# Who issues the last store of a chunked WKV kernel, and how its last logarithm is cut

## The chip, the core and the metric

The kernel runs on one core of one Trainium2 chip. The core has a matmul engine (TensorE, PE in the profile), a vector engine (VectorE, DVE), an activation engine (ScalarE, ACT), a general engine (GpSimd, POOL) and SyncE (SP), which here issues transfers and waits for them. Transfers between the on-chip memory and DRAM run on the core's 16 DMA engines; in this kernel SP, ACT and POOL all issue some. The metric is the device time of one execution in microseconds (us), lower is better.

## The reference

For each of 16 sequences and each of 256 channels a recurrence runs over 2048 steps. It keeps a weighted sum `aa` of values, a weighted sum `bb` of weights, and their common exponent `pp`:

```python
for t in range(seq_len):
    kk, vv = k[b, t, :], v[b, t, :]
    ww = u + kk
    qq = np.maximum(pp, ww)
    e1, e2 = np.exp(pp - qq), np.exp(ww - qq)
    output[b, t, :] = (e1 * aa + e2 * vv) / (e1 * bb + e2 + 1e-08)
    ww = pp - w + kk
    qq = np.maximum(ww, kk)
    e1, e2 = np.exp(ww - qq), np.exp(kk - qq)
    aa, bb, pp = e1 * aa + e2 * vv, e1 * bb + e2, qq
```

The output is a quotient, numerator over denominator, for every sequence, step and channel: 33.55 MB of float32, and as much again is read for each of `k` and `v`.

## The kernel before

**Tiling.** Time is cut into 16 chunks of 128 steps, and in each chunk the 16 sequences are taken four at a time. Such a piece of work, four sequences by 128 steps by 256 channels, is called a pair, since it is held as two halves `i` of two sequences each. There are `NP = 64` pairs, numbered in the order in which they run; the last one is 63. A tile of a pair has 128 partitions (steps) and 2 halves of 512 columns (two sequences by 256 channels).

**Stages of a pair.** `k` and `v` are loaded; matmuls form exponents in a PSUM tile `X` (lines 200 and 206), ScalarE takes exponentials (line 209), VectorE multiplies by `v` (line 218). Column sums go through a small state computation once per chunk, which carries the recurrence from chunk to chunk. Then the output side starts, and it is this side that the change touches:

- `DEN`: 12 matmuls (`apply`, line 321) form the denominator in a tile `X`, four for each of three terms, half 0 ahead of half 1 within each term.
- `LN`: `log_den` takes the logarithm of the whole tile on ScalarE (line 329) into a tile `rd`.
- `INV`: `inverse` takes exp(-x) of `rd` on ScalarE (line 337), which gives one over the denominator. `parts(n)` gives one slice with both halves for all pairs but the last, and two slices, one for each half, for pair 63.
- `NUM`: 12 more matmuls form the numerator, in a tile `num` or `X`.
- `MUL`: `mult` multiplies numerator and inverse on VectorE (line 349) into the output tile `ot`, again by `parts(n)`.
- `ST`: `store` issues, from SP, a transfer of half 0 (256 KB, line 362) and then a first piece of half 1 (128 KB, `piece`, line 355). Half 1 is stored in two pieces, since its two groups of 64 steps lie in swapped partitions.
- `SQ`: `store_rest` issues the second piece of half 1 (128 KB, also line 355). This step exists for pairs for which `shared(n)` is true, among them all from pair 52 on; for those the piece is issued by POOL.

**Order of the work.** The order of instructions on each engine is not left to a scheduler. Every step has a place on a common axis (the table `P`, with own entries under `TAIL` for the last ten pairs), steps are emitted by place as soon as those they name are done, and `K` keeps each engine's instructions in that order. In the last pairs ScalarE's order is strictly LN, INV of one pair, then LN, INV of the next.

**The end.** The program closes (line 478, where the tile context ends) with a drain instruction on each engine and a barrier: SP waits for the landing of all transfers, reports to a semaphore, and POOL, which has drained as the others have, waits for all reports, clears the semaphores and releases the engines.

Of the kernel before, what the change touches and what calls it, by code (L numbers as in the profile page):

```python
# [7 lines left out]
F32 = mybir.dt.float32  # L8
# [3 lines left out]
ACT = mybir.ActivationFunctionType  # L12
# [3 lines left out]
def kernel(  # L16
# [9 lines left out]
    K = tc.keep_in_program_order  # L26
    PE, DVE, SC, POOL, SP = nc.tensor, nc.vector, nc.scalar, nc.gpsimd, nc.sync
# [5 lines left out]
    D = 2 * Dm  # L33
    NP = 4 * NST
# [9 lines left out]
    RS = 2.0 ** -20  # L44
# [26 lines left out]
    rpool = ctx.enter_context(tc.tile_pool(name="rpool", bufs=NRD))  # L71
# [117 lines left out]
    X = [psx.tile([128, 2, D], F32, tag=f"X{a}", name=f"X{a}") for a in range(2)]  # L189
# [119 lines left out]
    RD, NUM, OT = {}, {}, {}  # L309
# [14 lines left out]
    def den(n, a):  # L324
        apply(X[a], n, ("S", "Id"), 1)

    def log_den(n, a):
        rd = rpool.tile([128, 2, D], F32, tag="rd", name="rd")
        K(SC.activation(rd, X[a], ACT.Ln, scale=RS))  # L329
        RD[n] = rd  # L330

    def parts(n):
        return (slice(0, 1), slice(1, 2)) if n == NP - 1 else (slice(0, 2),)

    def inverse(n):
        for i in parts(n):
            K(SC.activation(RD[n][:, i], RD[n][:, i], ACT.Exp, scale=-1.0))  # L337

    def by_x(n):
        return n >= NP - XT and n % 2 == 1  # L340
# [11 lines left out]
    def piece(n, h, queue):  # L352
        c, p = divmod(n, 4)
        t0 = c * TC + HS * (1 - h)
        K(queue.dma_start(out=out[4 * p + 2:4 * p + 4, t0:t0 + HS, :].rearrange("n t d -> t n d"), in_=OT[n][HS * h:HS * h + HS, 2:4, :]))
# [8 lines left out]
            piece(n, h, SP)  # L364

    def store_rest(n):
        piece(n, 1, POOL)


    ops, free = {}, {"K": NK, "KP": NKP, "V": NV, "N": 1, "RD": NRD, "OT": NOT, "VB": NVB}  # L370
# [5 lines left out]
    for n in range(NP):  # L376
# [24 lines left out]
        if j == 3:  # L401
            s = P["STATE"][0 if c == 0 else 2 if c == NST - 1 else 1]
            for i, (name, fn, *after) in enumerate((
# [5 lines left out]
                if not (name in ("SN", "KP") and c + 1 == NST):  # L409
                    step((name, c), n + s[i] - lead * SHARE, fn, (c,), after, mode=1)  # L410
        step(("DEN", n), place("DEN"), den, (n,), [("BK", c), ("DEN", n - 1), "mats"], "X", mode=3)
        step(("LN", n), place("LN"), log_den, (n,), [("DEN", n), ("INV", n - 1)], "RD", ["X"])
        step(("INV", n), place("INV"), inverse, (n,), [("LN", n)])
        step(("NUM", n), place("NUM"), num, (n,), [("BK", c), ("TV", n), ("NUM", n - 1), "mats"], "X" if by_x(n) else "N", mode=3)
        step(("MUL", n), place("MUL"), mult, (n,), [("NUM", n), ("INV", n), ("MUL", n - 1)], "OT", ["X" if by_x(n) else "N", "RD"])
        step(("ST", n), place("ST"), store, (n,), [("MUL", n), ("ST", n - 1)], None, [] if shared(n) else ["OT"])
        if shared(n):
            step(("SQ", n), place("SQ"), store_rest, (n,), [("ST", n)], None, ["OT"])
# [64 lines left out]
```

## Time and profile before

| what | us |
|---|---|
| median of 3 runs (lowest to highest) | 292.77 (292.13 to 294.27) |
| the profiled execution, its own time | 293.15 |
| its span, first to last instruction | 291.4 |
| time of the profiled execution outside the span | 1.75 |

The mean granted TensorE clock of the profiled execution is 0.992. All times inside the trace count from the start of the span. In the rows, a name like SPq or POOLq is an engine's sequencer, which issues transfers, waits and drains; L355 is line 355 of the kernel before. A row of a timeline or of the chain of waits begins with its start and its length in us. A row of a line's instructions has its shortest, median and longest duration in ns and then the starts of the first and last of them in us.

### The profile page before, as it was taken

The page shows a single profiled execution, that of the slowest core. Times are in us where ns is not written, and L with a number is a line of the kernel's source. Part 1 is how long each engine was busy: PE and PEld are TensorE (multiplying, and loading weights), DVE is VectorE, ACT ScalarE, POOL GpSimd, SP SyncE. Part 2 cuts the span into 40 slices and gives each one's busy share as a digit, 9 for nine tenths or more (in the row PEclk, how much of TensorE's full clock was granted, in tenths as well). Part 3 has the DMA queues.
Part 4 walks back from the last instruction along what each step waited for, and adds up shares of the span by engine and source line. Part 5 has one row for each costly group of instructions (what it writes and reads, how often), then busy time and mean ns, then how long its engine had stood idle before and what let it go on. Part 6 is the DMA issues. An engine that isn't in the chain of part 4 may idle for free.

```text
span 291.4 us, 8084 instructions
## 1 busy us (share of the span) xinstructions
PE 273.7 (94%) x3275; PEld 140.6 (48%) x3275; DVE 247.1 (85%) x423; ACT 258.4 (89%) x290; POOL 175.7 (60%) x218
## 2 busy tenths in 40 slices
PE   7999999999999999999999999999999999997750
PEld 7545744454545545444545455444545444544330
DVE  6575769989897989989898989899898989797860
ACT  1486398999999999999999999999999999997890
POOL 6177349575767687575767686675757674422230
PEclk9999999999999999999999999999999999999996
DMA  7999999999999999999999999999999999965885
GB/s 220 348 279 351 346 350 291 377 377 390 378 400 381 389 392 373 392 368 398 382 390 389 394 390 379 394 374 391 367 394 373 390 387 393 315 189 165 243 248 143
DMA packets 58550, 101.21 MB, mean 347 GB/s; under 512 B 5128, under 2 KB 43536, under 8 KB 58512
## 3 DMA queue, kind: packets, MB, share of 16 engines
q0 software_dynamic: 21216, 65.54, 65.0%
q1 hardware_dynamic: 37280, 35.14, 35.9%
q8 instruction: 25, 0.41, 0.6%
q14 instruction: 13, 0.11, 0.1%
q10 hardware_dynamic: 16, 0.01, 0.0%
HBM read 67.12 MB, written 33.55 MB: 345 GB/s over the span
## 4 chain that ended last, share of the span: by engine, by line
PE 71%; DMA 7%; DVE 5%; issue 5%; POOL 5%; ACT 4%; POOLq 0%; SPq 0%; ACTq 0%; DVEq 0%
PE X L206 17%; PE X L321 15%; PE num L321 12%; PE X L200 10%; PE TURN L148 9%; PE TOT L244 6%; DMA kf<-in_k_dram 4%; POOL vr L114 2%; DMA WUf<-in_u_dram 2%; PE TOT L257 2%; DVE ot L349 2%; POOL kr L110 2%; ACT EZR L209 1%; ACT rd L329 1%; DVE EZR L218 1%
## 5 line engine op out<-in xcount | busy, mean ns | idle before, releaser
L209 ACT ACTIVATE EZR<-X 128x1024 bf16<-128x1024 f32 x128 | 126.8, 1014 | 14.7 <-PE X L206 14.6
L213 POOL CAST vb<-vr 128x1024 bf16<-128x1024 f32 x54 | 56.3, 1043 | 70.9 <-DVE EZR L218 68.1
L218 DVE TENSOR_TENSOR EZR<-EZR,vb 128x2048 bf16<-128x2048 bf16 x64 | 77.9, 1219 | 0.4 <-ACT EZR L209 0.2
L349 DVE TENSOR_TENSOR ot<-num,rd 128x1024 f32<-128x1024 f32 x60 | 73.2, 1221 | 4.5 <-ACT rd L337 3.2
L337 ACT ACTIVATE rd<-rd 128x1024 f32<-128x1024 f32 (+1 forms) x65 | 67.9, 1046 | 2.0
L329 ACT ACTIVATE rd<-X 128x1024 f32<-128x1024 f32 x64 | 65.6, 1025 | 3.2 <-PE X L321 1.6
L148 PE MATMUL TURN<-Z 128*128 128x192 bf16 x331 | 57.0, 262 | 1.6 <-DVE Z L132 1.6
L114 POOL DMA_DIRECT2D vr<-in_v_dram x61 | 46.2, 758 | 13.8 <-DVE kr L193 7.1
L148 PEld LDWEIGHTS <-Z 128*128 128x128 bf16 x331 | 30.1, 102 | 49.0 <-issue 47.1
L200 PE MATMUL X<-WU,CO 64*64 64x512 bf16 x512 | 51.9, 390 | 0.9 <-DVE WU L175 0.6
L206 PE MATMUL X<-kr,NLE 128*128 128x512 f32 x128 | 45.6, 438 | 0.0
L206 PE MATMUL X<-kr,NLZ 128*128 128x512 f32 x128 | 45.5, 437 | 0.0
L107 POOL DMA_DIRECT2D kf<-in_k_dram x53 | 40.2, 758 | 0.0
L193 DVE CAST kr<-kf 128x1024 fp32r<-128x1024 f32 x39 | 31.9, 845 | 5.5 <-DMA kf<-in_k_dram 5.3
L200 PEld LDWEIGHTS <-CO 64*64 64x64 bf16 x512 | 15.7, 105 | 31.1 <-issue 26.2
L321 PE MATMUL X<-EZR,S 64*64 64x512 bf16 x256 | 26.2, 394 | 1.7 <-ACT rd L329 1.0
L321 PE MATMUL X<-cb,Id 64*64 64x512 bf16 x256 | 25.8, 376 | 0.0
L321 PE MATMUL X<-EZR,Id 64*64 64x512 bf16 x256 | 25.8, 376 | 0.0
L321 PE MATMUL num<-EZR,SN 64*64 64x512 bf16 x240 | 24.3, 386 | 1.5 <-DVE ot L349 1.5
L244 PE MATMUL TOT<-EZR,OH 128*32 128x256 bf16 x512 | 23.7, 277 | 0.7 <-DVE EZR L218 0.7
L321 PE MATMUL num<-cb,IdN 64*64 64x512 bf16 x240 | 24.0, 376 | 0.0
L321 PE MATMUL num<-EZR,IdN 64*64 64x512 bf16 x240 | 23.9, 376 | 0.0
(67 smaller groups left out, 268.9 us busy)
## 6 DMA issues: line engine op xcount, KB each, us to landing
vr<-in_v_dram POOLq DMA_DIRECT2D x61, 512.0 KB, 7.6
kf<-in_k_dram POOLq DMA_DIRECT2D x53, 512.0 KB, 8.5
out_dram<-ot SPq DMA_DIRECT2D x64, 256.0 KB, 9.1
out_dram<-ot SPq DMA_DIRECT2D x116, 128.0 KB, 9.7
kr<-in_k_dram POOLq DMA_DIRECT2D x8, 512.0 KB, 7.7
vr<-in_k_dram SPq DMA_DIRECT2D x3, 512.0 KB, 5.2
vr<-in_v_dram SPq DMA_DIRECT2D x3, 512.0 KB, 6.1
out_dram<-ot POOLq DMA_DIRECT2D x12, 128.0 KB, 3.1
```

Source lines behind the costliest of these rows:

```text
L114: K((SP if n < BYSP else POOL).dma_start(out=vr, in_=rows_of(v, n)))
L148: K(PE.matmul(TURN[:, 0:192], Z[:, 0:128], Z, start=first, stop=True, skip_group_check=True))
L200: K(PE.matmul(X[a][o:o + HS, i, :].rearrange("p (n d) -> p n d", n=2), CO[r:r + HS, q, :], WU[r:r + HS, :].unsqueeze(1).broadcast_to([HS, ...
L206: K(PE.matmul(X[a][:, i, :], (NLE, NLZ)[q], km[:, i, :], start=False, stop=True, skip_group_check=True))
L209: K(SC.activation(ez(n)[:, q, 1], X[a], ACT.Exp))
L213: K((DVE if n < EARLY else POOL).tensor_copy(vb, VR.pop(n)))
L218: K(DVE.tensor_mul(ez(n)[:, :, 0], ez(n)[:, :, 1], vb.unsqueeze(1).broadcast_to([128, 2, 2, D])))
L244: K(PE.matmul(t[32 * j:32 * j + 32, 0:256], OH[:, s:s + 32], ez(n)[:, 0, 1 - q, i, 256 * x:256 * x + 256], start=p == 0 and x == 0, stop=p ...
L321: K(PE.matmul(out_tile[o:o + HS, i, :], left, right, start=s == 0, stop=s == 2, tile_position=(r, o), skip_group_check=True))
L329: K(SC.activation(rd, X[a], ACT.Ln, scale=RS))
L337: K(SC.activation(RD[n][:, i], RD[n][:, i], ACT.Exp, scale=-1.0))
L349: K(DVE.tensor_mul(o.rearrange("p (i n) d -> p i (n d)", i=2)[:, i], NUM[n][:, i], RD[n][:, i]))
```

## The change

Two edits, both for pair 63 alone in their effect. The logarithm is taken by `parts(n)` too, and the exponential of half 0 is moved into the LN step, between the logarithms of the two halves; the INV step of pair 63 keeps the exponential of half 1. And the second piece of half 1 of pair 63 is issued by ScalarE's queue and no longer by POOL's. For all other pairs `parts(n)` has one slice, which ends at 2, so LN and INV emit what they emitted before.

```diff
-    def log_den(n, a):
-        rd = rpool.tile([128, 2, D], F32, tag="rd", name="rd")
-        K(SC.activation(rd, X[a], ACT.Ln, scale=RS))
-        RD[n] = rd
-
     def parts(n):
         return (slice(0, 1), slice(1, 2)) if n == NP - 1 else (slice(0, 2),)
 
+    def log_den(n, a):
+        RD[n] = rpool.tile([128, 2, D], F32, tag="rd", name="rd")
+        for i in parts(n):
+            K(SC.activation(RD[n][:, i], X[a][:, i], ACT.Ln, scale=RS))
+            if i.stop == 1:
+                invert(n, i)
+
+    def invert(n, i):
+        K(SC.activation(RD[n][:, i], RD[n][:, i], ACT.Exp, scale=-1.0))
+
     def inverse(n):
-        for i in parts(n):
-            K(SC.activation(RD[n][:, i], RD[n][:, i], ACT.Exp, scale=-1.0))
+        invert(n, parts(n)[-1])
...
     def store_rest(n):
-        piece(n, 1, POOL)
+        piece(n, 1, POOL if n < NP - 1 else SC)
```

## The prediction

> **What bounds the kernel now.** I read the page first, for what the whole kernel is limited by; then the chain of waits over the last 12 us, since both edits touch only the last pair; then the timeline there, and last the closing instructions at line 478.
>
> ```profile
> PE 273.7 (94%) x3275; PEld 140.6 (48%) x3275; DVE 247.1 (85%) x423; ACT 258.4 (89%) x290; POOL 175.7 (60%) x218
> ...
> out_dram<-ot SPq DMA_DIRECT2D x116, 128.0 KB, 9.7
> out_dram<-ot POOLq DMA_DIRECT2D x12, 128.0 KB, 3.1
> ```
>
> Over the span PE, ACT and DVE are all nearly full. None of that moves: one logarithm is cut in two, one store changes its issuer. The two store rows (median us from issue to landing) come back below as bounds.
>
> ```profile
> 281.83 1.39 issue
> 283.22 0.02 POOLq L355
> 283.24 0.60 POOL out_dram L355
> 283.84 1.01 issue
> 284.85 0.62 POOLq L478
> ```
>
> This is the end of the chain that ended last (start, length, what). It doesn't end with SP, which issues most stores, but with POOL: its last two stores at line 355, and then POOL's own instruction at line 478, the closing drain. So the question is what follows that drain.
>
> ```profile
> L478 SPq EVENT_SEMAPHORE  x11: 17/28/2897, 285.8 to 291.3; - x11
> L478 POOLq EVENT_SEMAPHORE  x4: 17/17/17, 290.7 to 291.3; - x4
> L478 POOLq DRAIN  x3: 46/93/5482, 284.8 to 291.1; - x3
> ...
> L478 ACTq DRAIN  x2: 14/595/1176, 282.6 to 290.9; - x2
> L478 DVEq DRAIN  x2: 19/413/807, 283.8 to 290.9; - x2
> ```
> ```profile
> L478 SPq DRAIN  x2: 7/7/7, 289.4 to 289.5; - x2
> ```
> ```profile
> SPq L478 <- DMA out_dram<-ot: 3.1, 2, 2.9
> SPq L478 <- PEq L478: 1.8, 2, 1.4
> ```
>
> The first block is line 478 over the whole run, the second the same line for SP between 289.4 and 290.0, the third SP's waits after 278. POOL's first drain starts at 284.8 and takes 5.48 us, to 290.3; ACT's takes 1.18 from 282.6 and DVE's 0.81 from 283.8, both long over. SP waits 2.9 us for landings, drains at 289.5 and has reported; then it waits 1.4 us for the barrier. The row names PEq there, but PE was done at 282; the last reporter was POOL, whose first barrier instruction comes at 290.7, 0.4 after its drain ended. From there to the end of the span it is 291.4 - 290.7 = 0.7 us. So **POOL's drain sets the end, 1.2 us behind SP** (290.7 - 289.5), and SP is set by the landing of the last store.
>
> **The stores of the last pair.** The timeline of that stretch, and for three stores their time from issue to landing:
>
> ```profile
> 280.62 1.06 ACT L337 ACTIVATE rd<-rd 128x1024 f32<-128x1024 f32 x1
> ...
> 281.59 1.01 ACT L329 ACTIVATE rd<-X 128x1024 f32<-128x1024 f32 x1
> 281.71 1.23 DVE L349 TENSOR_TENSOR ot<-num,rd 128x1024 f32<-128x1024 f32 x1 [0.78 <-ACT rd L337]
> 281.72 0.41 PE L321 MATMUL X<-cb,IdN 64*64 64x512 bf16 x4
> 282.62 1.15 ACT L337 ACTIVATE rd<-rd 128x512 f32<-128x512 f32 x2
> ...
> 283.23 0.60 POOL L355 DMA_DIRECT2D out_dram<-ot  x1 [1.40 <-DVE ot L349]
> 283.29 1.29 DVE L349 TENSOR_TENSOR ot<-X,rd 128x512 f32<-128x512 f32 x2 [0.35 <-ACT rd L337]
> 283.39 0.59 SPq L355 DMA_DIRECT2D out_dram<-ot  x1
> 284.08 0.54 SPq L362 DMA_DIRECT2D out_dram<-ot  x1
> 284.72 1.01 SPq L355 DMA_DIRECT2D out_dram<-ot  x1
> 284.87 0.60 POOL L355 DMA_DIRECT2D out_dram<-ot  x1 [1.03 <-DVE ot L349]
> ```
> ```profile
> L337 ACT ACTIVATE rd<-rd x2: 613/622/631, 282.6 to 283.2; 128x512 f32<-128x512 f32 x2
> ```
> ```profile
> L355 SPq DMA_DIRECT2D out_dram<-ot x1: 1012/1012/1012, 284.7 to 284.7; - x1
> ...
> DMA to landing us min/median/max: 4.4/4.4/4.4
> ```
> ```profile
> L355 POOL DMA_DIRECT2D out_dram<-ot x1: 603/603/603, 284.9 to 284.9; - x1
> ...
> DMA to landing us min/median/max: 3.9/3.9/3.9
> ```
> ```profile
> L355 POOL DMA_DIRECT2D out_dram<-ot x1: 603/603/603, 283.2 to 283.2; - x1
> ...
> DMA to landing us min/median/max: 3.3/3.3/3.3
> ```
>
> Pair 63's pieces land at 284.7 + 4.4 = 289.1 (SP's) and 284.9 + 3.9 = 288.8 (POOL's). SP's closing report at 289.5 is 0.4 behind the later one.
>
> **Edit one, the logarithm by halves.** Removed is one ACT instruction of 1.01 us, added are two of half the size. No row has that shape; bounds are 0.50 (half of 1.01) and 0.61 (the exponential of that shape). I take 0.57: the half exponential of 0.61 less the 0.05 by which the full logarithm (1.01) is shorter than the full exponential (1.06). A dependent successor starts 282.62 - 281.59 = 1.03 after its producer, 0.02 behind its end; an independent one 0.54 after (the pair ends at 282.62 + 1.15 = 283.77, its second starts 0.61 earlier, at 283.16). New ACT order: Ln 0 from 281.59 to 282.16 (its matmuls cannot let it start sooner, ACT is in the previous exponential until then); Exp 0 from 282.18 to 282.79; Ln 1 from 282.72 to 283.29; Exp 1 from 283.31 to 283.92. Exp 0 ends 0.45 sooner than now (282.62 + 0.61 = 283.24), Exp 1 0.15 later (283.77).
>
> The earlier Exp 0 lets VectorE multiply half 0 from 282.94, where its previous multiplication ends (281.71 + 1.23), and not from 283.29: 0.35 gained. But who waits for half 0 is SP's 256 KB store, and SP is in the previous pair's piece until 283.39 + 0.59 = 283.98, just where the multiplication ends now (283.29 + half of 1.29, about 283.95). It issues at 284.08 either way, so **this gain is worth 0.0**; the cover is SP's own queue. Half 1 is multiplied at about 283.97 and is done near 284.65, 0.07 later than now (283.29 + 1.29 = 284.58). SP's next issue, at 284.72, is still bound by its own 256 KB issue, so it costs nothing there: 0.0. Only the ScalarE store sees the 0.07.
>
> **Edit two, the store.** POOL loses its issue of 0.60 at 284.87, and its drain can start behind its store of pair 62, at about 283.2. What sets the drain's 5.48 us isn't in any row by itself. If it runs from the last issue on POOL, it ends at 283.2 + 5.5 = 288.7; if it follows the landing of POOL's last store (288.8) by 290.3 - 288.8 = 1.5, it ends at 283.2 + 3.3 + 1.5 = 288.0. Both are ahead of SP's 289.5, so the barrier would then wait for SP. ACT gains one issue, behind its last exponential; nothing is queued behind it but ACT's drain.
>
> The store itself: ready at 284.65, it is issued at about 284.7 from ACT, 0.2 ahead of POOL's. Its landing is the unknown. The only issues from ACT are two at the start:
>
> ```profile
> L121 ACTq DMA_DIRECT2D WUf<-in_w_dram x1: 1096/1096/1096, 1.2 to 1.2; - x1
> L121 ACTq DMA_DIRECT2D WUf<-in_u_dram x1: 513/513/513, 2.4 to 2.4; - x1
> ```
>
> Nearest is SP's store of the same shape, issued at the same time in the same stretch: 4.4 to landing, so 289.1, which leaves the last landing where it is. Upper end: ACT's store queues behind SP's, begins when that issue ends (285.7) and takes 4.4, so 290.1. For the lower end, the transfers after 285:
>
> ```profile
> q1 hardware_dynamic: 561, 0.52, 25.5%
> q0 software_dynamic: 85, 0.22, 17.7%
> ```
>
> Per MB, POOL's queue (q0) kept the 16 engines busy for 17.7 / 0.22 = 80% of these 6.4 us, SP's (q1) for 25.5 / 0.52 = 49%. Moving 0.131 MB saves 0.131 x 0.31 x 6.4 = 0.26 us of transfer time, so the last landing could come at 288.8. I take 289.1, the row in the same state. The Trainium skill, in "DMA: Bandwidth & Descriptors", section Latency and other measured facts, gives about 600 ns to the first byte for a store issued by SP or ACT and about 1 us for one issued by GpSimd; by that the landing would be some 0.4 us earlier than POOL's. The rows here don't bear that out: with the queues full SP's 128 KB took 4.4 and POOL's 3.9.
>
> **Sum**, on the profiled execution: SP reports at 289.1 + 0.4 = 289.5, POOL's barrier instruction then comes at 289.5 and not at 290.7, and the rest takes 0.7. Edit one 0.0, edit two -1.2 us. If the 0.4 that POOL needed between drain and barrier recurs, -0.8; with the last landing at 288.8, -1.5; at 290.1, -0.2. The profiled execution would take 293.15 - 1.2 = 291.95; on the median, 292.77 - 1.2 = 291.6.
>
> **Rivals.** *The drain isn't tied to POOL's own store.* If it ends a fixed time behind the last landing of any store (290.3 - 289.1 = 1.2 here), moving one store doesn't help: the span stays at 291.4 and the time at 292.8 (from 292.5 to 293.8 with the last landing between 288.8 and 290.1). For it: there is one long drain in this trace, and its end follows both. Against it: SP's drains took 7 ns, and ACT's 1.18 and DVE's 0.81 are about what the work still running on them needed (1.15 for ACT's two exponentials), so drains look like waits for an engine's own work. The same page of the Trainium skill, section Issuing engines are not separate DMA queues, speaks for this outcome: transfers interleave on the same engines whoever issues them, and another issuer saves only the sequencer's time to start them. By that rule no more than POOL's issue of 0.60 would be at stake; no row here tests it.
>
> *The new store lands late, and SP becomes slower than the drain was.* ACT's and SP's stores are both of the kind called hardware_dynamic. SP's last issues already swell from 0.59 to 1.01 us, which looks like a full queue. If ACT's store lands after 290.3, that is over 5.6 us from its issue, the end is later than now. The row of the busy kernel, 9.7 us for SP's 128 KB, would put it at 284.7 + 9.7 = 294.4, the end at 294.4 + 0.4 + 0.7 = 295.5 and the time at 292.77 + 4.1 = 296.9. Against it: that median holds loads beside the stores, and of the three stores at the end shown above none took over 4.4.
>
> *The halved logarithm does what it is shaped for* and half 0's store starts 0.35 earlier. It would need SP free at 283.6; the row at 283.39 says it isn't. Even so it is worth at most 0.35 more, a time of 291.2, and it is counted with the forecast.
>
> **How the numbers follow.** A change under about 1% (2.9 us) is what measurements of this kernel can't tell from none. Forecast, POOL's drain off the end, 0.7: 291.6, with -1.5 to -0.2 giving 291.3 to 292.6. Drain not tied, 0.2: 292.8. Late landing, 0.08, of which half between 292.8 and 295.7 and half beyond. Something unseen that gains over 2.9: 0.02. The medians move too: the lowest of the three runs before lies 0.6 below its median, so the range goes from 291.3 - 0.6 = 290.7 to 293.0, a little past the second case. Faster by over 1% 0.02, slower by over 1% 0.04, within 1% 0.94.
>
> **What would show it.** In the trace of the changed kernel POOL's first drain starts near 283.2 and ends before SP's; SP's last wait at line 478 shrinks from 1.4 to near nothing; SP issues at 284.1 and 284.7 as now; DVE starts half 0 near 282.9. A drain of POOL that still ends over 1 us behind SP's would show the second case, a landing of ACT's store after 290 the third.

## The result and the profile after

Over 20 runs each, the changed kernel took 291.89 us (291.0 to 292.73) and the kernel before 292.5 us (291.75 to 294.27), both medians. The ratio is 0.9964, with a 95% interval of 0.9952 to 0.9975: about 1.05 us less (0.73 to 1.40). That is below the 1% which the prediction took for the least that can be told from nothing, but here the interval leaves 1 out. The ratio isn't the quotient of the two medians: these are only 0.61 us apart (0.9979), and the means of the runs 0.90 (0.9969). In a second comparison, on another occasion with 12 runs of the changed kernel, the ratio was 0.9985 (0.9964 to 1.0007). The forecast was 291.6, with a range of 290.7 to 293.0.

The profiled execution took 291.12, and its span is 2.0 us shorter than that of the one before. This is more than the change did, as the timeline of the end shows (start, length, engine, line and operation; the rows of PE and PEld are left out):

```profile
span 289.4 us, 8085 instructions
```
```profile
280.44 0.58 ACT L333 ACTIVATE rd<-X 128x512 f32<-128x512 f32 x1
280.56 1.22 DVE L353 TENSOR_TENSOR ot<-num,rd 128x1024 f32<-128x1024 f32 x1 [0.78 <-ACT rd L338]
281.05 0.63 ACT L338 ACTIVATE rd<-rd 128x512 f32<-128x512 f32 x1
281.58 0.58 ACT L333 ACTIVATE rd<-X 128x512 f32<-128x512 f32 x1
281.71 0.69 DVE L353 TENSOR_TENSOR ot<-X,rd 128x512 f32<-128x512 f32 x1
281.81 0.38 SPq L366 DMA_DIRECT2D out_dram<-ot  x1
282.08 0.60 POOL L359 DMA_DIRECT2D out_dram<-ot  x1 [1.39 <-DVE ot L353]
282.19 0.63 ACT L338 ACTIVATE rd<-rd 128x512 f32<-128x512 f32 x1
282.24 0.60 SPq L359 DMA_DIRECT2D out_dram<-ot  x1
282.86 0.69 DVE L353 TENSOR_TENSOR ot<-X,rd 128x512 f32<-128x512 f32 x1 [0.46 <-ACT rd L338]
282.93 0.55 SPq L366 DMA_DIRECT2D out_dram<-ot  x1
283.58 0.60 SPq L359 DMA_DIRECT2D out_dram<-ot  x1
283.58 0.75 ACTq L359 DMA_DIRECT2D out_dram<-ot  x1
```

The last pair's logarithm starts at 280.44, where it started at 281.59 before. These 1.15 us come from earlier work that the change leaves as it was: over the 14 profiles of this study that start lies anywhere from 280.40 to 282.78. So the comparison goes by the **closing stretch**, from that start to the end of the span: 291.40 - 281.59 = 9.81 us before, 289.41 - 280.44 = 8.97 after, which is 0.84 less. "Behind the logarithm" below means from that start.

The closing instructions, line 482 of the changed kernel, over the whole run, then SP's alone from 288.1 to 288.3:

```profile
L482 POOLq EVENT_SEMAPHORE  x4: 17/17/17, 288.2 to 289.3; - x4
L482 POOLq DRAIN  x3: 46/249/5066, 282.1 to 289.1; - x3
...
L482 ACTq DRAIN  x2: 8/259/510, 284.4 to 288.5; - x2
```
```profile
L482 SPq DRAIN  x2: 7/7/7, 288.1 to 288.2; - x2
```

POOL's drain now starts at 282.1 and is over at 287.1, 1.1 us ahead of SP, which reports at 288.2; POOL's first barrier instruction follows at once, at 288.2. The chain of waits no longer ends with POOL but with the last multiplication (the first block, start and length), and SP's own waits, after 276, have changed places (the second block: total, times, longest):

```profile
282.83 0.02 issue
282.86 0.69 DVE ot L353
```
```profile
...
SPq L482 <- DMA out_dram<-ot: 3.4, 3, 1.6
SPq L482 <- PEq L482: 1.1, 2, 0.9
```

There are two waits for the barrier. The first, in which SP waited 1.4 us for POOL's drain, is down to 1.1 - 0.9 = 0.2. The second, for the release, was 1.8 - 1.4 = 0.4 and is now 0.9: half a microsecond is given back there. The end is SP's, and SP's is the landing of the last stores, here SP's and ScalarE's last piece and POOL's store of pair 62:

```profile
L359 SPq DMA_DIRECT2D out_dram<-ot x1: 596/596/596, 283.6 to 283.6; - x1
...
DMA to landing us min/median/max: 4.1/4.1/4.1
```
```profile
L359 ACTq DMA_DIRECT2D out_dram<-ot x1: 752/752/752, 283.6 to 283.6; - x1
...
DMA to landing us min/median/max: 4.2/4.2/4.2
```
```profile
L359 POOL DMA_DIRECT2D out_dram<-ot x1: 603/603/603, 282.1 to 282.1; - x1
...
DMA to landing us min/median/max: 3.5/3.5/3.5
```

ScalarE's store lands at 283.6 + 4.2 = 287.8, 7.4 behind the logarithm; before, the last landing came 7.5 behind it. POOL's own last store lands at 285.6, and its drain ends 1.5 to 1.6 us later.

### The profile page after: what moved, and what is told of

Read it like the earlier page. It is cut to its first block, busy times and chain, and to the rows that moved or that the text cites. A ratio compares the mean times of both kernels' runs of the same rounds, so it can differ in the third digit from the quotient of the medians.

```text
span 289.4 us, 8085 instructions
## 1 busy us (share of the span) xinstructions
PE 273.8 (95%) x3275; PEld 141.1 (49%) x3275; DVE 247.6 (86%) x423; ACT 258.3 (89%) x291; POOL 175.4 (61%) x217
## 4 chain that ended last, share of the span: by engine, by line
PE 85%; ACT 6%; DVE 3%; issue 2%; DMA 1%; SPq 0%; DVEq 0%
PE X L206 21%; PE X L321 15%; PE TURN L148 14%; PE num L321 13%; PE X L200 12%; PE TOT L244 7%; ACT rd L333 2%; ACT EZR L209 2%; PE TOT L257 2%; ACT rd L338 2%; DVE ot L353 1%; PE TURN L301 1%; DMA out_dram<-ot 1%; DVE EZR L218 1%; DVE AB L287 0%
## 5 line engine op out<-in xcount | busy, mean ns | idle before, releaser
L333 ACT ACTIVATE rd<-X 128x1024 f32<-128x1024 f32 (+1 forms) x65 | 65.7, 1011 | 2.5 <-PE X L321 0.9
```

What stands on the lines that cost most here:

```text
L333: K(SC.activation(RD[n][:, i], X[a][:, i], ACT.Ln, scale=RS))
```

## The experiments

Each ratio is against the kernel before, run beside it; below 1 is faster. Diffs are against the kernel before or the changed one, as named. The table gives, from each trace, times behind the logarithm: the landing of POOL's own last store, the end of POOL's long drain, the last landing of any store, SP's report (the start of its drain that reports), and the end of the span.

| kernel | POOL's landing | drain's end | last landing | SP reports | end |
|---|---|---|---|---|---|
| before | 7.14 | 8.75 | 7.49 | 7.87 | 9.81 |
| changed | 5.12 | 6.69 | 7.38 | 7.76 | 8.97 |
| changed, again | 4.97 | 6.53 | 7.53 | 7.91 | 9.10 |
| edit two alone | 4.79 | 6.36 | 7.21 | 7.59 | 8.78 |
| edit one alone | 7.06 | 8.66 | 7.31 | 7.69 | 9.74 |
| last store by SP | 5.65 | 7.21 | 7.58 | 7.90 | 9.11 |
| pair 62's piece by SP, halved log | 2.80 | 4.32 | 6.86 | 7.12 | 8.32 |
| the same, whole log | 3.39 | 4.92 | 7.12 | 7.39 | 8.60 |
| both last pieces by POOL | 7.99 | 9.64 | 7.99 | 8.61 | 10.77 |
| pair 62 by POOL | 8.26 | 9.86 | 8.68 | 9.12 | 10.93 |
| SP free, halved log | 6.30 | 7.90 | 7.43 | 7.87 | 9.04 |
| SP free, whole log | 6.78 | 8.38 | 7.44 | 7.89 | 9.51 |
| last six pairs by SP, trailing | before the stretch | before the stretch | 7.88 | 8.38 | 9.15 |
| last six pairs by SP, in order | before the stretch | before the stretch | 7.15 | 7.66 | 8.42 |

**One part at a time.** Edit two alone, against the kernel before:

```diff
     def store_rest(n):
-        piece(n, 1, POOL)
+        piece(n, 1, POOL if n < NP - 1 else SC)
```

> Edit two alone: ScalarE issues the last store, the logarithm of the last pair stays whole. Measured from the start of the last pair's logarithm to the end of the span, the stretch was 9.8 us before and is 9.0 with both edits. Theory (the closing drain of POOL ends about 1.6 us behind the landing of POOL's own last store, and the barrier waits for the later of that drain and SP's report, 0.4 behind the last landing): the whole gain is edit two's; half 1 is even ready 0.1 sooner. Stretch 8.9 to 9.0, ratio 0.996. Rival (the gain comes from half 0 being ready 0.35 sooner, through the halved logarithm): stretch 9.4 to 9.8, ratio 0.999 to 1.000.

The ratio is 0.9954 (0.9933 to 0.9974), and the closing stretch, 8.78, is a little shorter than expected. Edit one alone, the changed kernel with the store given back:

```diff
-        piece(n, 1, POOL if n < NP - 1 else SC)
+        piece(n, 1, POOL)
```

> Edit one alone: halved logarithm, the last store stays with POOL. Theory: POOL's drain again ends about 1.6 us behind its last landing and sets the end; half 1 is ready 0.1 later, so the stretch is 9.8 to 10.0 and the ratio 1.000 to 1.0005. Rival (halved logarithm carries the gain): stretch 9.0 to 9.4, ratio 0.996 to 0.998.

The ratio is 1.0005 (0.9987 to 1.0024), the closing stretch 9.74, just under the 9.8 expected. POOL's drains in the two, edit two alone first:

```profile
L478 POOLq DRAIN  x3: 46/242/4734, 282.4 to 289.3; - x3
```
```profile
L482 POOLq DRAIN  x3: 46/93/5277, 284.7 to 290.8; - x3
```

With edit one alone the drain ends at 284.7 + 5.3 = 290.0 of a span of 291.1, as before the change; with edit two alone at 287.1 of 289.5. The gain is edit two's, and edit one adds none to it.

**Who issues the store.** The changed kernel, with SP in ScalarE's place:

```diff
-        piece(n, 1, POOL if n < NP - 1 else SC)
+        piece(n, 1, POOL if n < NP - 1 else SP)
```

> Both edits, but the last store is SP's and not ScalarE's. Theory: POOL's drain leaves the end as in the changed kernel (1.6 us behind the landing of pair 62's store, ahead of SP's report); SP's third issue in a row starts 0.6 to 1.0 us later than ScalarE's did, so the last landing comes 0.0 to 0.6 later. Stretch 9.0 to 9.6, ratio 0.996 to 0.9985. Rival (what counts is that ScalarE issues it on a queue of its own): stretch 9.8 or more, ratio 1.000 or more.

The ratio is 0.9967 (0.9945 to 0.9988). SP's third issue in a row starts 0.65 later than ScalarE's did and takes 1.87 us, and still the last landing is only 0.2 later than in the changed kernel (0.05 later than in its second profile). What matters is that the store isn't POOL's.

**The drain follows its own engine's store.** Pair 62's second piece is SP's too:

```diff
-        piece(n, 1, POOL if n < NP - 1 else SC)
+        piece(n, 1, POOL if n < NP - 2 else SP if n < NP - 1 else SC)
```

> As the changed kernel, and pair 62's second piece is issued by SP too, so that POOL's last store is pair 61's, 2 us earlier. Theory: POOL's drain ends 1.6 us behind that store's landing, some 2 us sooner than in the changed kernel, and this gains nothing, since SP's report sets the end; SP's queue has one issue of 0.6 more ahead of the last pair, so its last stores start 0.6 later: stretch 9.0 to 9.6, ratio 0.996 to 0.9985. Rival (the drain ends behind the last landing of any store): its end stays within 2 us of the last landing and doesn't move ahead with POOL's own last store. If the drain's length instead runs from POOL's last issue, its end lies 4.4 to 4.9 behind that issue's end, whatever the landing.

The ratio is 0.9956 (0.9939 to 0.9973). POOL's drain, and its last store, that of pair 61:

```profile
L482 POOLq DRAIN  x3: 93/194/4698, 280.4 to 288.6; - x3
```
```profile
L359 POOL DMA_DIRECT2D out_dram<-ot x1: 603/603/603, 280.4 to 280.4; - x1
...
DMA to landing us min/median/max: 3.2/3.2/3.2
```

The store lands at 283.6 and the drain ends at 285.1, 1.5 later, while stores of SP and ScalarE are in flight until 287.6. That is against the first rival of the prediction, which tied the drain to the last landing of any store. It is against a fixed length from POOL's last issue too: the drain ends 4.07 behind the end of that issue, where such a length gave 4.4 to 4.9. One part of the expectation missed: the last landing came 0.5 sooner than in the changed kernel, not later, and the stretch is 8.32, not 9.0 to 9.6. SP's extra piece was emitted behind the last pair's stores and not ahead of them, and POOL's store of pair 62 no longer ran beside them. With a whole logarithm the ratio is the same:

> Whole logarithm; ScalarE issues the last store, SP the second piece of pair 62. This is the earlier run with pair 62's piece on SP, without the halved logarithm. Theory (the halved logarithm makes half 1 0.1 later and gives nothing back): stretch 8.1 to 8.3 against 8.3 there, ratio 0.994 to 0.996. Rival (the halved logarithm was worth something once POOL is out of the way): stretch 8.5 or more.

0.9955 (0.9938 to 0.9972), with a closing stretch of 8.60 where up to 8.3 was expected and the rival had 8.5 or more. It is 0.28 longer than with the halved one, and the last landing 0.26 later, although half 1 was multiplied 0.11 sooner. By its stretch the rival is right, but in this trace the stores ahead already landed late (pair 62's 256 KB at 4.32 against 3.85), and the ratios don't part the two. So it stays undecided.

**The cost doubled.** The changed kernel, with both pieces of the last pair's half 1 by POOL:

```diff
         for h in range(1 if shared(n) else 2):
-            piece(n, h, SP)
+            piece(n, h, SP if n < NP - 1 else POOL)
...
-        piece(n, 1, POOL if n < NP - 1 else SC)
+        piece(n, 1, POOL)
```

> The suspected cost doubled: halved logarithm, and both pieces of half 1 of the last pair issued by POOL. Theory (POOL's drain ends 1.5 to 1.6 us behind the landing of POOL's own last store): the second piece is issued some 0.6 later than POOL's only one was, lands 0.4 to 1.0 later, and the drain with it; SP is done before and waits. Stretch from the last pair's logarithm to the end 10.1 to 10.9 (9.8 before), ratio 1.001 to 1.004. Rival (the length of the drain isn't tied to the number or landing of POOL's stores): stretch 9.7 to 9.9, ratio 1.000.

The ratio is 1.0031 (1.0017 to 1.0046), slower as expected, but the edit did more than it was meant to. POOL's stores in the timeline:

```profile
284.78 2.39 POOL L359 DMA_DIRECT2D out_dram<-ot  x4 [5.16 <-DVE ot L353]
```

Four stores stand in a row, after POOL had waited 5.16 us. By the table `P` a second piece is emitted nearly three pairs behind the first one (places 11.7 apart, 4.0 from pair to pair; an expectation below says four pairs), so the last pair's first piece went ahead of the second pieces of pairs 61 and 62 on POOL's queue and held them up. The size is therefore not that of one store. The rule holds: the last of the four lands at 7.99, the drain ends 1.65 later and sets the end, while SP had reported at 8.61.

The same happened in the kernel that was to free SP, with pair 62's first piece by POOL:

```diff
-            piece(n, h, SP)
+            piece(n, h, POOL if n == NP - 2 else SP)
```

> As the changed kernel, and both pieces of half 1 of pair 62 are issued by POOL, so that SP is free when half 0 of the last pair is ready. Theory: now the halved logarithm shows, SP issues half 0 about 0.5 sooner (2.0 behind the logarithm's start and not 2.5); but half 1 is ready no sooner, its pieces issue at 3.1 as before, POOL's drain ends near 7.4 behind its second store, and with one more store on POOL's costlier queue the last landing comes at 7.2 to 7.6: stretch 8.8 to 9.3, ratio 0.996 to 0.998, no gain over the changed kernel. Rival (SP's queue was what hid a real gain): stretch 8.5 or less, ratio 0.9945 or less.

The ratio is 1.0039 (1.0025 to 1.0054), where 0.996 to 0.998 was expected. POOL again issued four stores in a row, and the last landings came late (POOL's 3.8 to 4.9 us from issue, SP's and ScalarE's 5.4 and 5.5). It says nothing on the logarithm, and the drain still ended 1.60 behind POOL's last landing.

**Is the halved logarithm worth something once SP is free?** For a clean answer POOL's stores from pair 54 on were emitted with their pair's others, in order, and pair 62's half 1 went to POOL whole. Against the changed kernel, and in the same way against one with a whole logarithm:

```diff
-        for h in range(1 if shared(n) else 2):
-            piece(n, h, SP)
+        for h in range(1 if shared(n) and n < NP - 10 else 2):
+            piece(n, h, ((POOL if n == NP - 2 else SP) if h == 0 else (SC if n == NP - 1 else POOL)) if n >= NP - 10 else SP)
...
-        if shared(n):
+        if shared(n) and n < NP - 10:
```

> As the changed kernel (halved logarithm, last store by ScalarE), with the first piece of pair 62's half 1 moved from SP to POOL, and POOL's stores from pair 54 on emitted in order of the pairs, which the earlier run of this kind had upset. SP is then free when half 0 of the last pair is ready. Theory: SP issues half 0 at 2.0 and not at 2.5, but half 1 is ready no sooner, so the last landing stays at 7.1 to 7.5; POOL's last store, issued at about 2.3, lands at 5.5 to 6.0 and its drain ends at 7.1 to 7.6, no later than SP's report: stretch 8.7 to 9.2, ratio 0.996 to 0.9975, within 0.2 us of the same kernel with a whole logarithm. Rival (the halved logarithm gains once SP is free): 0.35 us shorter than the same kernel with a whole logarithm.

> The same arrangement of stores with a whole logarithm. Theory: half 0 issues at 2.4, the pieces of half 1 at 3.0 to 3.1; stretch within 0.2 us of the run with the halved one, ratio 0.996 to 0.9975. Rival: 0.35 us longer than that run.

The ratios are 0.9991 (0.997 to 1.0012) and 0.9998 (0.9974 to 1.0021), which don't part them and are both above what was expected. SP did issue half 0 sooner, at 1.99 with the halved logarithm and 2.42 with the whole one, and the last landing is the same, 7.43 and 7.44: half 0 isn't what lands last. The closing stretch nevertheless differs by 0.47, on the rival's side. The table says where: POOL's last store, issued at 2.24 in both, landed at 6.30 and at 6.78, and its drain, at 7.90 and 8.38, came level with SP's report in the one and 0.5 behind it in the other. Both landings are later than the 5.5 to 6.0 expected. A later half 0 may have run into POOL's store; one trace of each doesn't show it. In the changed kernel POOL's drain ended 1.1 ahead of SP's report, so a sooner end of that drain would gain nothing there.

**POOL out of the last six pairs.** A whole logarithm, ScalarE for the last store and SP for the second pieces of pairs 58 to 62, first through the step as it is:

```diff
-        piece(n, 1, POOL)
+        piece(n, 1, POOL if n < NP - 6 else SP if n < NP - 1 else SC)
```

> Whole logarithm; ScalarE issues the last store, and SP issues the second pieces of pairs 58 to 62, which POOL did. With pair 62's alone on SP the last landing came 0.5 sooner than in the changed kernel. Theory (POOL's stores take the DMA engines longer for the same bytes and hold SP's up): with none of them in the last 10 us SP's stores land 2.4 to 3.4 after issue, the stretch is 8.0 to 8.4 and the ratio 0.993 to 0.996. Rival (three issues a pair, 1.6 us of every 2.0, fill SP's queue): SP falls behind, issues take over 1 us and the ratio is 0.998 or more.

The ratio is 0.999 (0.9971 to 1.001), and the theory missed (the stretch is 9.15, where 8.0 to 8.4 was expected): SP had two of those pieces left behind the last pair's stores and issued its last at 5.33. With each piece emitted beside its pair's others, as above:

> Whole logarithm; SP issues the second pieces of pairs 58 to 62, each right behind its pair's other stores (in the earlier run they trailed four pairs behind and came last of all), and ScalarE the last store. Theory (POOL's costlier stores held the others up; POOL's drain is long over): SP's half 0 of the last pair at 3.1 behind the logarithm's start and its last piece at 3.7, landings 2.9 to 3.4 later, so at 6.6 to 7.1: stretch 8.1 to 8.5, ratio 0.994 to 0.996. Rival (three issues a pair keep SP behind): its last issue at 4.3 or later, stretch 8.8 or more, ratio 0.997 or more.

The ratio is 0.9971 (0.9949 to 0.9994), short of what was expected and where the rival had it, though the closing stretch, 8.42, is the theory's and the last landing, 7.15, just past its upper end. The closing instructions of this kernel, POOL's over the whole run and SP's from 289.5 to 289.8:

```profile
span 290.4 us, 8081 instructions
```
```profile
L478 POOLq DRAIN  x3: 46/93/5034, 273.4 to 290.1; - x3
```
```profile
L478 SPq DRAIN  x2: 7/7/7, 289.6 to 289.6; - x2
```
```profile
SPq L478 <- PEq L478: 0.6, 2, 0.5
```

POOL's long drain was over at 278.5, and of SP's two waits for the barrier, in the last row, the longer is 0.5. From SP's report to the end it takes 290.4 - 289.6 = 0.8 us, where the changed kernel took 289.4 - 288.2 = 1.2.

**The changed kernel beside these three:**

> The changed kernel once more, beside the three others on the same chip. Expected: ratio 0.995 to 0.9975, stretch 8.8 to 9.1, POOL's drain ending 1.5 to 1.6 behind the landing of its own last store, and the pause of about 0.35 us on POOL somewhere behind the drain.

The ratio is 0.9985 (0.9964 to 1.0007), above what was expected, with the closing stretch, 9.10, at its upper end. The gain in the two closing stretches is 0.84 and 0.71 us, 0.29% and 0.24% of the time; the intervals of the two ratios, a saving of 0.25 to 0.48% and of -0.07 to 0.36%, overlap about there.

## Why the prediction was right, point by point

**POOL's drain sets the end: right.** Giving POOL's last store to another engine, without edit one, gives the whole gain (0.9954), leaving it with POOL gives none (1.0005), and a drain pushed later makes the kernel slower (1.0031).

**What the drain follows: two answers were left open, and the second holds.** The first was a fixed length from POOL's last issue, the second a fixed time behind the landing of POOL's last store. In the 12 traces with POOL's last store in or near the stretch, the drain ends 1.52 to 1.65 us behind the landing of POOL's own last store, and 1.36 in the two where that store was issued over eight us ahead of the stretch. From the end of that store's issue to the drain's it takes anything from 3.84 to 5.83 us in the 12.

**The halved logarithm is worth 0.0 here: right.** Its steps came as worked out: half a logarithm took 0.58 where 0.57 was taken, half 0 was multiplied from 1.27 behind the logarithm (282.94 in the prediction is 1.35) and not from 1.70, and SP issued it at 2.49 in both traces, held by the piece of pair 62. Half 1 was multiplied 0.11 later, against 0.07 expected. With POOL's store gone from the end, edit one still adds no gain: with edit two alone the stretch is 8.78, with both edits 8.97 and 9.10.

**ScalarE's store lands with SP's: right.** 4.2 us from its issue, where 4.4 was taken from SP's row; the late landing of the second rival didn't come. It landed no faster after issue than POOL's had (3.9). The saving of 0.4 us that the Trainium skill's "DMA: Bandwidth & Descriptors", section Latency and other measured facts, led to is not seen: ScalarE's store landed 7.38 behind the logarithm, POOL's had landed at 7.14.

**The sum's last term was mis-sized.** "The rest takes 0.7" was read from POOL's first barrier instruction of the trace before. After, SP's report came 7.76 behind the logarithm, 0.1 sooner than before, but from there to the end it took 1.21. The term stands at 1.19 to 1.21 in all six traces (of five kernels) where SP reports over 0.5 us after the drain's end and POOL stored for pair 61 or later, and at 0.76 to 0.77 in the two where POOL's last store was pair 57's. These are POOL's closing instructions from its first barrier instruction to its next drain, in the changed kernel (from 288.2 to 289.0) and in the kernel with the last six pairs by SP, in order, from 289.6 to 289.95:

```profile
L482 POOLq EVENT_SEMAPHORE  x2: 17/17/17, 288.2 to 288.3; - x2
L482 POOLq DRAIN  x1: 249/249/249, 288.7 to 288.7; - x1
```
```profile
L478 POOLq EVENT_SEMAPHORE  x2: 17/17/17, 289.7 to 289.7; - x2
L478 POOLq DRAIN  x1: 93/93/93, 289.8 to 289.8; - x1
```

From the second barrier instruction to the drain it takes 0.4 us in the first kernel and 0.1 in the other. The 0.4 between drain and barrier, which the prediction let recur as its -0.8 case, did recur, at another place: a pause of 0.32 to 0.37 in POOL's closing instructions, once in each of the six traces, with the drain next to it longer (249 ns in the changed kernel's row, 93 in the other). So, with what was measured put in, the sum is -1.2 less 0.1 plus 0.45, about -0.85, which is the closing stretch's 0.84.

**The drain isn't tied to POOL's own store: this rival didn't come.** POOL's drain moved with its own store and left the last landing behind, and moving one store did help. The Trainium skill's "DMA: Bandwidth & Descriptors", section Issuing engines are not separate DMA queues, says that another issuer saves only the sequencer's time. For the transfers of this change the traces agree with it: the last landing moved by 0.1. The gain of 0.84 in the closing stretch wasn't in the transfers but in POOL's drain, which no longer ends last. When pair 62's piece left POOL too, the last landing came sooner by another 0.5 with the halved logarithm and 0.1 with the whole one, in one trace each; what did that isn't shown.

**A better version** wasn't established. The kernel with edit two alone and both with pair 62's piece on SP have ratios of 0.9954 to 0.9956, with intervals that hold the changed kernel's 0.9964. Their closing stretches are 0.2 to 0.65 shorter than its 8.97, in one profile each.

## What to carry to other kernels

Read what ends last, down to the closing drains and the barrier: in the kernel before 1.2 us passed between SP's report and POOL's, the last. Ask of each engine not only when its last work ends but how long its drain then lasts, and give the last transfer to an engine whose drain doesn't wait for it. Making an early half ready sooner was worth nothing here, where its store waited for SP's queue and the other half landed last.

## What the hardware showed that was not expected

Drains differ by engine. ScalarE's drain in the changed kernel took 0.51 us from 284.4 and was over 2.9 us before its own store landed at 287.8; POOL's lasted until 1.4 to 1.65 us after its store's landing in all 14 traces. Whether this goes with the engine or with the kind of its transfers isn't separated: POOL's stores run as software_dynamic, SP's and ScalarE's as hardware_dynamic, in all of these kernels. Closing behind recent POOL stores took another 0.45 us, in the pause above and the longer drain beside it. These traces show no cause for the pause. It falls right behind the long drain, or up to four closing instructions later. It is gone in the two kernels where POOL's last store was issued some 16 us ahead of the barrier, though still there where that was 8 us.
